# Moving the operand products of experts 1 and 2 and ScalarE's first copies ahead, and splitting a second stage of product 2 a third time

## The chip, the cores and the metric

The kernel runs on one core of a Trainium2 chip. The metric is device time in microseconds (us) of one execution; the median of several runs is compared. A profile of one execution comes with it.

The engines are named as the profile names them: PE is TensorE (matmul), DVE VectorE, ACT ScalarE, POOL GpSimd, SP SyncE. GpSimd and SyncE do little but issue transfers here, GpSimd those that cast float32 to float16.

## The reference

```python
"x": (16, 512, 512), "router_logits": (16, 512, 8), "expert_weights": (8, 512, 2048)   # float32
...
probs = np.exp(router_logits - logits_max)
probs = probs / np.sum(probs, axis=-1, keepdims=True)
for e in range(8):
    output += probs[:, :, e:e+1] * np.matmul(x, expert_weights[e])
```

A softmax over eight experts weighs eight matrix products of 8192 rows. Written as one product, row t of the left operand is the concatenation of p[t, e] * x[t] over the experts, 8 x 512 = 4096 long, and the right operand is the weights of all experts stacked, 4096 x 2048.

## The kernel before, in words

**Levels.** The big product is done in Strassen's way (Winograd's form), in up to three levels. The outer level splits the rows into even and odd blocks of 256, the experts into 0 to 3 and 4 to 7, and the columns into two halves of 1024; it makes seven products of the right operands (called product 1 to 7) for each of 16 pairs of row blocks. The inner level splits each of those again into seven steps, in the order 1, 5, 6, 2, 7, 3, 4; a step is eight matmuls of 128x128 weights by 128x512. The third level is used in some stages only: two such products are taken together (class `Third`), and steps 1 and 5 of both, 32 matmuls of 512 columns, become 14 parts of four matmuls of 256 columns. Its operands are sums that VectorE makes: `s`, four sums of 128x1024 from the left operands of both products, and `t`, sums of the weights, made once (class `Split`).

**Stages.** The work is cut into stages of two products each. Product 1 fills stages 0 to 4 and half of 5 to 8, product 2 the rest up to stage 14, and so on. A stage is split a third time where the program calls `third(stage, r)`: before the change stages 2, 3, 4 (product 1), stage 10 (product 2) and six stages of product 3. In such a stage TensorE does x1 x5 q1 q5, a step held over from the stage before, x2 q2 x6 q6, another one, x7 q7 x3 q3 x4 q4, and then the other steps. Of the third level's part 5, ScalarE copies the left 256 columns into a second bank and the right 256 into a tile `t5`, which VectorE adds back after parts 6 and 7.

**Operands and results.** The left operand z is xT * pT on VectorE, in float16; d are sums of z for the inner level, in a pool of three buffers (`spool`, tag "d"). Weights are cast by POOL's queue (L126) into `wpool`, 15 tiles. PSUM has eight banks, taken in turn by `bank()`. Results and copies of banks go through `hpool`, 13 tiles. SyncE's queue (L123) loads and stores.

**What sets the order.** VectorE and ScalarE always run in the order of the program. TensorE, POOL and SyncE do so from the place where `ordered[0]` is set, just ahead of stage 0; for what stands before it, a scheduler may interleave the instructions. In the stages a queue of VectorE's tasks is worked off by a planner with costs (`later(cost, make)`): TensorE's clock advances by 1.73 us a step, and tasks that a step needs are pulled forward.

**The start.** The first four half blocks of rows do not wait for transposed x: TensorE makes their operand itself. `diag_e(e)` (VectorE, L112) multiplies the identity by the probabilities of expert e, `early_z0(e, d, js)` multiplies x by those diagonals, 16 matmuls of 128x128 for one expert, into one bank for each j, and `evacuate` copies the banks out (VectorE at L238 for even j, ScalarE at L236 for odd). Then two column blocks (the loop over n) each take 64 matmuls, 16 for each of the four experts, into four banks, which ScalarE copies into h tiles (L335) and SyncE stores to `kept`. In the second block `early_xp1` makes transposes of further rows (matmuls by `ident`) and their probabilities (by `ones`). `softmax_of_all` makes the probabilities of all rows on VectorE, with one exponential on ScalarE (L184) and two casts there (L294, L295), and stores them to `p_dram`, from where the stages load pT.

The weights of the two column blocks come through POOL's queue in the order expert 0 (in two halves), 1, 2, 3 of the first block, experts 0 and 1 of the second, two blocks of x, and experts 2 and 3 of the second.

Of the kernel before, what the change touches and what calls it, by code (L numbers as in the profile page):

```python
# [31 lines left out]
def kernel(  # L32
# [7 lines left out]
    nc = tc.nc  # L40
    P = 128
    f16 = mybir.dt.float16
    f32 = mybir.dt.float32
# [4 lines left out]
    E, _, EH = expert_weights.shape  # L48
# [6 lines left out]
    HQ = 256  # L55
    NHQ = T // HQ
# [9 lines left out]
    spool = ctx.enter_context(tc.tile_pool(name="spool", bufs=3))  # L66
# [7 lines left out]
    def h_tile(shape, dtype):  # L74
        return hpool.tile(shape, dtype, name="h", tag="h")

    def half():
        return h_tile([P, NB], f32)
# [10 lines left out]
    with tc.tile_pool(name="psum0", bufs=1, space=bass.MemoryType.PSUM) as psum0:  # L89
        zero = wpool.tile([P, NB], f16, name="zero", tag="w")  # L90
# [9 lines left out]
    def note(i):  # L100
        last[i.ins.engine] = i.ins
        if ordered[0]:
            tc.keep_in_program_order(i)
# [5 lines left out]
    act = dve  # L109

    def tt(o, a, b, op):
        dve(nc.vector.tensor_tensor(out=o, in0=a, in1=b, op=op))  # L112
# [9 lines left out]
    def sp(o, i):  # L122
        note(nc.sync.dma_start(out=o, in_=i))  # L123
# [4 lines left out]
    def bank():  # L128
        return psum.tile([P, NB], f32, name="ps", tag="ps")

    def mm(ps, z, w, start, stop):
        note(nc.tensor.matmul(ps, z, w, start=start, stop=stop, skip_group_check=True))  # L132
# [3 lines left out]
    def new_w():  # L136
        return wpool.tile([P, K8, NB], f16, name="w", tag="w")
# [31 lines left out]
    def inner_sums(b, t7=None):  # L169

        w = {1: b[0, 0], 2: b[1, 0], 3: b[1, 1], 7: t7 or b[0, 1]}

        def step(p, x, y):
            if p not in w:
                w[p] = new_w()
            tt(w[p], x, y, SUB)
        return w, {5: lambda: step(5, b[0, 1], b[0, 0]), 6: lambda: step(6, b[1, 1], w[5]),
                   4: lambda: step(4, b[1, 0], w[6]), 7: lambda: step(7, b[1, 1], b[0, 1])}

    def softmax(lg, J, pf):  # L180
        mx = h_tile([P, J], f32)
        dve(nc.vector.tensor_reduce(out=mx, in_=lg, axis=AX, op=mybir.AluOpType.max))  # L182
        tt(lg, lg, mx.unsqueeze(2).to_broadcast([P, J, E]), SUB)
        nc.scalar.activation(out=lg, in_=lg, func=mybir.ActivationFunctionType.Exp)  # L184
        sm = h_tile([P, J], f32)
        dve(nc.vector.tensor_reduce(out=sm, in_=lg, axis=AX, op=ADD))  # L186
        dve(nc.vector.reciprocal(out=sm, in_=sm))  # L187
        n = pf.shape[1]
        tt(pf, lg.rearrange("p j e -> p e j")[:, 0:n], sm.unsqueeze(1).to_broadcast([P, n, J]), MUL)
        return pf  # L190
# [27 lines left out]
    def early_p(t):  # L218
        if t == 0:
            return softmax(lg0[t], 4, cpool.tile([P, HE, 4], f16, name="ph0"))  # L220
        pf = softmax(lg0[t], 4, cpool.tile([P, HE, 4], f32, name="pf0"))
        odd = pf.rearrange("p e (q j) -> p e q j", j=2)[:, :, :, 1]
        tt(odd[:, 0:2], odd[:, 0:2], odd[:, 2:4], ADD)
        ph = cpool.tile([P, HE, 4], f16, name="ph1")
        dve(nc.vector.tensor_copy(ph, pf))
        return ph

    def diag(p):

        d = h_tile([P, 4, P], f16)  # L230
        tt(d, ident.unsqueeze(1).to_broadcast([P, 4, P]), p.to_broadcast([P, 4, P]), MUL)
        return d

    def evacuate(o, ps, i):
        if i % 2:
            act(nc.scalar.copy(o, ps))  # L236
        else:
            dve(nc.vector.tensor_copy(o, ps))  # L238
# [4 lines left out]
    def diag_e(e):  # L243
        return diag(ph0[0][:, e].unsqueeze(2))

    def early_z0(e, d, js=range(4)):
        for j in js:
            ps = bank()
            for c in range(C):
                mm(ps[:, ds(c * P, P)], xs0[:, j, ds(c * P, P)], d[:, j], c == 0, c == C - 1)  # L250
            evacuate(z0[j][:, e], ps.rearrange("p (c t) -> p c t", c=C), j)
# [5 lines left out]
    def diag_j(j):  # L257
        return diag(ph0[1][:, :, ds(j % 4, 1)])

    def early_xp1(j, d):  # L260
        t, rows = j // 2 - 2, ds(j % 2 * P, P)
        ps = bank()
        for c in range(C):
            mm(ps[:, ds(c * P, P)], xs0[:, j, ds(c * P, P)], ident, c == 0, c == C - 1)
        evacuate(xp1[t][0][:, :, rows], ps.rearrange("p (c t) -> p c t", c=C), 0)
        ps = bank()
        mm(ps, ones, d.rearrange("p e t -> p (e t)"), True, True)
        evacuate(xp1[t][1][:, :, rows], ps.rearrange("p (e t) -> p e t", e=HE), 1)

    R = 4  # L270
    J = HQ // R
    p_dram = dram.tile([NHQ, 3 * HE, HQ], f16, name="p_dram")
# [3 lines left out]
    def load_logits():  # L276
        dve(nc.vector.memset(lg_all[:, 0, 0:1], 0.0))
        dve(nc.vector.memset(lg0[1][:, 0, 0:1], 0.0))
        for q in range(2):
            sp(lg0[1][:, ds(2 * q, 2), :], lg_f[ds((4 + 2 * q) * HQ, HQ)].rearrange("(j p) e -> p j e", p=P))  # L280
        for r in range(R):
            sp(lg_all[ds(r * NHQ, NHQ)], lg_v[r])

    def softmax_of_all():

        pf = softmax(lg_all, J, h_tile([P, E, J], f32))
        pq = h_tile([P, HE, J], f32)
        tt(pq, pf[:, 0:HE], pf[:, HE:E], ADD)
        low = ds(P // 2, P // 2)
        pv = pf.rearrange("p (s e) j -> p s e j", s=2)[low]  # L290
        tt(pv[:, :, 0:2], pv[:, :, 0:2], pv[:, :, 2:4], ADD)
        tt(pq[low, 0:2], pq[low, 0:2], pq[low, 2:4], ADD)
        ph = h_tile([P, 3 * HE, J], f16)
        act(nc.scalar.copy(ph[:, 0:E], pf))  # L294
        act(nc.scalar.copy(ph[:, E:], pq))  # L295
        for r in range(R):
            sp(p_dram[:, :, ds(r * J, J)], ph[ds(r * NHQ, NHQ)])

    kept = [dram.tile([2, HQ, NB], f32, name=f"kept_{i}") for i in range(NI)]

# [2 lines left out]
    ORDERS = [(c, j) for c in range(C) for j in range(4)], QUARTERS  # L303

    ds_ = [diag_e(0)]
    for h in range(2):
        early_z0(0, ds_[0], (2 * h, 2 * h + 1))
        for i in range(3 - 2 * h):
            mm(bank(), zero[:, 0:P], zero, True, True)
    load_logits()  # L310
    ds_ += [diag_e(1), diag_e(2)]
    for n in range(2):
        ps = [bank() for _ in range(4)]
        for e in range(HE):
            if n == 0 and e == 1:
                ds_.append(diag_e(3))
            if n == 0 and e == 2:
                ph0.append(early_p(1))
                ds_ = [diag_j(j) for j in range(4, 8)]
                softmax_of_all()  # L320
                w, sums = inner_sums(b11, new_w())
            for c, j in ORDERS[n == 0 and e == 0]:
                mm(ps[j], z0[j][:, e, c], b11[e // 2, n][:, e % 2 * C + c, :],
                   e + c == 0, e == HE - 1 and c == C - 1)
                ahead = {(0, 1, 3): 1, (0, 3, 3): 2, (1, 3, 3): 3}.get((e, c, j))
                if n == 0 and ahead:
                    early_z0(ahead, ds_[ahead])
            if n == 1:
                for j in ((4, 5), (6, 7), (), ())[e]:
                    early_xp1(j, ds_[j - 4])  # L330
                if e == 1:
                    sums[5]()
        for j in range(4):
            o = half()
            act(nc.scalar.copy(o, ps[j]))  # L335
            sp(kept[j // 2][n].rearrange("(p j) m -> j p m", j=2)[j % 2], o)

    ordered[0] = True
    SLOT = 1.73
# [37 lines left out]
    def evacuated(cost=0.61):  # L377
        clock["dve"] = max(clock["dve"], clock["pe"]) + cost
# [240 lines left out]
    class Third:  # L619
# [25 lines left out]
        def part(self, p, m):  # L645
            n = "xq"[THIRD.index(p)]
            if m == 1:
                self.b.banks[n] = bank()
            ya, yb = self.a.banks.get(n), self.b.banks[n]
            z, w = self.op(p, m), self.split.op(p, m)  # L650
            o = {1: (yb, 0), 5: (yb, 1), 2: (ya, 0), 6: (yb, 0), 7: (yb, 0), 3: (ya, 1), 4: (yb, 0)}[m]
            for c in range(C):
                mm(o[0][:, COLS[o[1]]], z[:, c], w[:, c], m == 1 and c == 0, c == C - 1)
            clock["pe"] += 0.44
            if m == 5:
                ya = self.a.banks[n] = bank()
                act(nc.scalar.copy(ya[:, COLS[0]], yb[:, COLS[0]]))
                self.t5[n] = h_tile([P, HQ], f32)
                act(nc.scalar.copy(self.t5[n], yb[:, COLS[1]]))
            elif m in (6, 7):  # L660
                evacuated(0.35)
                tt((ya if m == 6 else yb)[:, COLS[1]], yb[:, COLS[0]], self.t5[n], ADD)
# [552 lines left out]
    for stage in (2, 3, 4):  # L1215
        third(stage, 1)
    at(1, 2, splits[1].queue)
    for stage in (10,):
        third(stage, 2)
    at(9, 2, splits[2].queue)  # L1220

# [50 lines left out]
```

## Time and profile before

| | |
|---|---|
| median of three runs | 1371.24 us (1371.21 to 1373.33) |
| the profiled execution | 1371.77 us |
| its span in the trace | 1369.9 us |
| PE busy | 1360.8 us, 99% |
| DVE busy | 1122.1 us, 82% |
| POOL busy | 407.3 us, 30% |
| ACT busy | 194.7 us, 14% |
| chain that ended last | PE 98% |

The span runs from the first to the last recorded instruction of the profiled execution; 1.87 us of its time lie outside. Busy shares are averages over stages with different limits, so the rows that matter are those of the start and of single stages: what each engine did there and what ended its idle time.

### The profile page before, as it was taken

What the parts mean: (1) busy time and instruction counts of PE and PEld (TensorE: products, weight loads), DVE (VectorE), ACT (ScalarE), POOL (GpSimd) and SP (SyncE); (2) the same over time, 40 slices, a digit from 0 to 9 for tenths busy, and PEclk for the clock granted to TensorE, in tenths of its full rate; (3) what the DMA queues carried; (4) which work ended last, traced back from release to release, by engine and by line L of the source; (5) the groups of instructions that cost most, each with busy time, mean ns of one, the idle gap of its engine ahead of it and who ended that gap; (6) DMA issues with size and microseconds to landing.
All of it is one profiled execution on the core that took longest, in us unless ns stands there. A gap on an engine that the chain in (4) does not pass through costs nothing.

```text
span 1369.9 us, 18108 instructions
## 1 busy us (share of the span) xinstructions
PE 1360.8 (99%) x6634; PEld 645.9 (47%) x6634; DVE 1122.1 (82%) x1359; ACT 194.7 (14%) x358; POOL 407.3 (30%) x644
## 2 busy tenths in 40 slices
PE   8999999999999999999999999999999999999998
PEld 4455544454444444444444444444444444456554
DVE  5875867789889888788887888888889797898873
ACT  3232211100001111111111100000000000123221
POOL 3123324231223232333323122232332422223232
PEclk9999999999999999999999999999999999999999
DMA  9999999999897999999999978988798979989996
GB/s 181 205 239 230 249 241 280 289 289 367 265 327 231 335 327 306 256 286 310 306 271 343 339 257 222 210 240 203 228 256 222 247 203 291 306 205 239 208 204 119
DMA packets 191945, 353.79 MB, mean 258 GB/s; under 512 B 52976, under 2 KB 87024, under 8 KB 186736
## 3 DMA queue, kind: packets, MB, share of 16 engines
q0 software_dynamic: 88048, 183.02, 56.3%
q1 hardware_dynamic: 98048, 129.63, 31.0%
q10 hardware_dynamic: 5760, 39.99, 7.9%
q8 instruction: 52, 0.85, 0.3%
q14 instruction: 37, 0.30, 0.1%
HBM read 211.85 MB, written 167.97 MB: 277 GB/s over the span
## 4 chain that ended last, share of the span: by engine, by line
PE 98%; DVE 1%; DMA 1%; ACT 0%; issue 0%; POOL 0%; DVEq 0%; POOLq 0%
PE ps L132 98%; DMA w<-in_expert_weights_dram 1%; DVE h L112 0%; POOL w L126 0%; DVE z L112 0%; DVE z L238 0%; DVE h L186 0%; DVE h L187 0%; DVE h L182 0%; ACT h L184 0%; ACT h L294 0%; ACT h L335 0%; ACT h L1209 0%; DVE pf L112 0%; DVE ps L112 0%
## 5 line engine op out<-in xcount | busy, mean ns | idle before, releaser
L132 PE MATMUL ps<-w,z 128*128 128x512 f16 x5256 | 1131.2, 375 | 2.4 <-DMA w<-in_expert_weights_dram 2.4
L132 PEld LDWEIGHTS <-z 128*128 128x128 f16 x5336 | 521.9, 98 | 604.1 <-DVE h L112 2.7
L126 POOL DMA_DIRECT2D out_dram<-h x380 | 249.3, 663 | 746.2 <-ACT h L578 364.4
L112 DVE TENSOR_TENSOR h<-ps,h 128x512 f32<-128x512 f32 x415 | 284.5, 688 | 187.7 <-PE ps L132 169.8
L112 DVE TENSOR_TENSOR z<-xT,pT 128x2048 f16<-128x2048 f16 x216 | 262.2, 1217 | 6.6 <-DMA xT<-w 4.8
L132 PE MATMUL ps<-w,d 128*128 128x512 f16 x880 | 199.1, 379 | 0.0
L132 PEld LDWEIGHTS <-d 128*128 128x128 f16 x880 | 86.1, 98 | 101.7
L112 DVE TENSOR_TENSOR z<-z,d 128x2048 f16<-128x2048 f16 x110 | 131.5, 1217 | 0.0
L578 ACT COPY h<-ps 128x512 f32<-128x512 f32 x64 | 37.5, 586 | 503.7 <-PE ps L132 499.2
L112 DVE TENSOR_TENSOR w<-w 128x1024 f16<-128x1024 f16 (+2 forms) x88 | 99.9, 1146 | 1.8 <-PE ps L132 1.0
L567 ACT COPY h<-ps 128x512 f32<-128x512 f32 x90 | 52.7, 586 | 309.2 <-PE ps L132 297.1
L112 DVE TENSOR_TENSOR ps<-ps,h 128x512 f32<-128x512 f32 (+1 forms) x106 | 62.2, 591 | 23.8 <-PE ps L132 23.2
L112 DVE TENSOR_TENSOR d<-z 128x1024 f16<-128x1024 f16 x110 | 74.6, 687 | 4.2 <-PE ps L132 2.8
L564 ACT COPY h<-ps 128x512 f32<-128x512 f32 x90 | 51.9, 589 | 142.0 <-PE ps L132 132.4
L126 POOL DMA_DIRECT2D kept<-h x56 | 30.9, 552 | 102.6 <-ACT h L567 74.3
L126 POOL DMA_DIRECT2D w<-in_expert_weights_dram x65 | 48.8, 782 | 20.1 <-DMA wd<-w 8.4
L126 POOL DMA_DIRECT2D wd<-w x78 | 44.3, 593 | 32.9 <-DVE w L112 27.6
L112 DVE TENSOR_TENSOR u<-xT,pT 128x2048 f16<-128x2048 f16 x38 | 46.2, 1217 | 0.0
L112 DVE TENSOR_TENSOR h<-h 128x512 f32<-128x512 f32 (+2 forms) x69 | 45.1, 675 | 0.1
L112 DVE TENSOR_TENSOR z<-z,u 128x2048 f16<-128x2048 f16 x34 | 41.4, 1217 | 0.1
L560 ACT COPY ps<-ps 128x512 f32<-128x512 f32 x45 | 25.6, 570 | 99.6 <-PE ps L132 93.8
L112 DVE TENSOR_TENSOR z<-z 128x2048 f16<-128x2048 f16 x32 | 39.1, 1222 | 0.7
(61 smaller groups left out, 278.7 us busy)
## 6 DMA issues: line engine op xcount, KB each, us to landing
out_dram<-h POOLq DMA_DIRECT2D x380, 256.0 KB, 6.9
pT<-p_dram SPq DMA_DIRECT2D x125, 256.0 KB, 6.8
h<-kept SPq DMA_DIRECT2D x108, 256.0 KB, 7.2
w<-wd ACTq DMA_DIRECT2D x25, 1024.0 KB, 8.9
xT<-x SPq DMA_DIRECT2D x74, 256.0 KB, 6.8
w<-in_expert_weights_dram POOLq DMA_DIRECT2D x35, 512.0 KB, 9.9
wd<-w POOLq DMA_DIRECT2D x64, 256.0 KB, 6.5
h<-out_dram SPq DMA_DIRECT2D x60, 256.0 KB, 5.4
```

Source lines behind the costliest of these rows:

```text
L112: dve(nc.vector.tensor_tensor(out=o, in0=a, in1=b, op=op))
L126: note(nc.gpsimd.dma_start(out=o, in_=i, **how))
L132: note(nc.tensor.matmul(ps, z, w, start=start, stop=stop, skip_group_check=True))
L560: act(nc.scalar.copy(self.banks["b"], x))
L564: act(nc.scalar.copy(o[tn], q if p == 5 else x))
L567: act(nc.scalar.copy(o[TN[p]], b if p == 2 else x))
L578: act(nc.scalar.copy(o[tn], b))
```

## The change

1. `early_z0` of experts 1 and 2, with the diagonals, moves ahead of the first column block; before, each expert's 16 matmuls stood between matmuls of the block. Those of expert 3 move to the place before expert 1's matmuls of the block. One filler matmul on zeros is left out (three stay).
2. `early_p(1)`, the next diagonals and `softmax_of_all` move from ahead of expert 2 to ahead of expert 1 of the first block. `softmax_of_all` now returns a function, `keep`, with ScalarE's two casts and SyncE's four stores to `p_dram`; it is called after the first block's four bank copies and stores, so that these come first on ScalarE and on SyncE.
3. Stage 11 is split a third time as stage 10 is.
4. `t5` is no longer taken from `hpool`, one tile for each of two banks, but from the pool of "d", as one tile with both halves. This holds for every stage that is split a third time.

```diff
         ph = h_tile([P, 3 * HE, J], f16)
-        act(nc.scalar.copy(ph[:, 0:E], pf))
-        act(nc.scalar.copy(ph[:, E:], pq))
-        for r in range(R):
-            sp(p_dram[:, :, ds(r * J, J)], ph[ds(r * NHQ, NHQ)])
+
+        def keep():
+            act(nc.scalar.copy(ph[:, 0:E], pf))
+            act(nc.scalar.copy(ph[:, E:], pq))
+            for r in range(R):
+                sp(p_dram[:, :, ds(r * J, J)], ph[ds(r * NHQ, NHQ)])
+        return keep
...
     ds_ = [diag_e(0)]
-    for h in range(2):
-        early_z0(0, ds_[0], (2 * h, 2 * h + 1))
-        for i in range(3 - 2 * h):
-            mm(bank(), zero[:, 0:P], zero, True, True)
+    early_z0(0, ds_[0], (0, 1))
+    for i in range(3):
+        mm(bank(), zero[:, 0:P], zero, True, True)
+    ds_.append(diag_e(1))
+    early_z0(0, ds_[0], (2, 3))
     load_logits()
-    ds_ += [diag_e(1), diag_e(2)]
+    for e in (1, 2):
+        ds_.append(diag_e(e + 1))
+        early_z0(e, ds_[e])
     for n in range(2):
         ps = [bank() for _ in range(4)]
         for e in range(HE):
             if n == 0 and e == 1:
-                ds_.append(diag_e(3))
-            if n == 0 and e == 2:
+                early_z0(3, ds_[3])
                 ph0.append(early_p(1))
                 ds_ = [diag_j(j) for j in range(4, 8)]
-                softmax_of_all()
+                keep_p = softmax_of_all()
                 w, sums = inner_sums(b11, new_w())
             for c, j in ORDERS[n == 0 and e == 0]:
                 mm(ps[j], z0[j][:, e, c], b11[e // 2, n][:, e % 2 * C + c, :],
                    e + c == 0, e == HE - 1 and c == C - 1)
-                ahead = {(0, 1, 3): 1, (0, 3, 3): 2, (1, 3, 3): 3}.get((e, c, j))
-                if n == 0 and ahead:
-                    early_z0(ahead, ds_[ahead])
...
             sp(kept[j // 2][n].rearrange("(p j) m -> j p m", j=2)[j % 2], o)
+        if n == 0:
+            keep_p()
...
-                self.t5[n] = h_tile([P, HQ], f32)
+                if not self.t5:
+                    t = spool.tile([P, 2, HQ], f32, name="d", tag="d")
+                    self.t5 = {"x": t[:, 0], "q": t[:, 1]}
...
-    for stage in (10,):
+    for stage in (10, 11):
         third(stage, 2)
```

## The prediction

> **What bounds the kernel now.** I read the page first, then TensorE's waits, then the timelines of the start and of stages 10 and 11.
>
> ```profile
> PE 1360.8 (99%) x6634; PEld 645.9 (47%) x6634; DVE 1122.1 (82%) x1359; ACT 194.7 (14%) x358; POOL 407.3 (30%) x644
> PE 98%; DVE 1%; DMA 1%; ACT 0%; issue 0%; POOL 0%; DVEq 0%; POOLq 0%
> ```
> ```profile
> PE ps L132 <- ACT h L335: 1.4, 1, 1.4
> PE ps L132 <- DVE ps L112: 0.2, 1, 0.2
> ```
>
> TensorE is busy 1360.8 us of a span of 1369.9 us and carries 98% of the chain that ended last. Only two things can shorten this kernel: less matmul time, and the waits at the start. Behind the start TensorE waits once, 0.2 us for VectorE, so what the start gains stays gained unless something later takes it back.
>
> Timelines of the start (start, duration, engine, form, count, idle before and its releaser): first TensorE, then VectorE and ScalarE.
>
> ```profile
> 7.53 0.38 PE L132 MATMUL ps<-zero 128*128 128x512 f16 x1
> 10.28 1.89 PE L132 MATMUL ps<-w,z 128*128 128x512 f16 x8 [2.37 <-DMA w<-in_expert_weights_dram]
> ...
> 18.97 1.06 PE L132 MATMUL ps<-h,w 128*128 128x128 f16 x16
> 19.86 10.52 PE L132 MATMUL ps<-w,z 128*128 128x512 f16 x48
> 31.76 0.38 PE L132 MATMUL ps<-ident,w 128*128 128x128 f16 x4 [1.37 <-ACT h L335]
> ...
> 37.04 8.15 PE L132 MATMUL ps<-w,z 128*128 128x512 f16 x37
> ```
> ```profile
> 7.51 0.69 DVE L238 CAST z<-ps 128x512 f16<-128x512 f32 x1 [0.70 <-PE ps L132]
> 8.13 0.69 DVE L112 TENSOR_TENSOR h<-ident,ph 128x512 f16<-128x512 f16 x1
> ...
> 20.60 0.18 DVE L182 TENSOR_REDUCE h<-lg 128x4 f32<-128x32 f32 x1
> ```
> ```profile
> 30.21 0.62 ACT L294 CAST h<-h 128x512 f16<-128x512 f32 x1 [3.37 <-DVE h L112]
> 31.04 2.04 ACT L335 COPY h<-ps 128x512 f32<-128x512 f32 x4
> ```
>
> Two idle stretches stand out: 2.37 us before the first weights, and the one before 31.76, where early_xp1 needs a bank that ScalarE has not copied out. The 48 matmuls from 19.86 are issued by 30.22 (48 x 0.2158 us, the pitch of 96 matmuls in 20.72 us in the stage rows below), so that gap is 1.54 us. ScalarE's copies begin only at 31.04, since the casts of the softmax stand ahead of them and wait for VectorE's chain, which began at 20.60.
>
> **The start, step by step.** One expert's early_z0 is 16 matmuls, 19.86 - 18.97 = 0.89 us of TensorE. Those of experts 1 and 2 now run in the idle stretch. Expert 1's diagonals (one VectorE operation of 0.69) come between expert 0's two casts and are done by the second one's start at 7.51; expert 2's, now at 8.13, are done at 8.8. So expert 1 runs 7.55 to 8.44 and expert 2 8.87 to 9.76, before 10.28. This takes 2 x 0.89 = 1.78 us off the path. The filler that goes (7.53) lies in idle time: nothing. Expert 3's 0.89 us only moves, to behind expert 0's block.
>
> Late next could be the weights. The casting queue shows when a block lands, by when it wakes (its idle, and the block that released it):
>
> ```profile
> 11.73 0.76 POOL L126 DMA_DIRECT2D w<-in_expert_weights_dram  x1 [0.57 <-DMA w<-in_expert_weights_dram]
> 14.47 0.74 POOL L126 DMA_DIRECT2D w<-in_expert_weights_dram  x1 [1.98 <-DMA w<-in_expert_weights_dram]
> 17.59 0.70 POOL L126 DMA_DIRECT2D w<-in_x_dram  x1 [2.38 <-DMA w<-in_expert_weights_dram]
> 21.09 0.71 POOL L126 DMA_DIRECT2D w<-in_x_dram  x1 [2.80 <-DMA w<-in_expert_weights_dram]
> 23.29 0.71 POOL L126 DMA_DIRECT2D w<-in_x_dram  x1 [1.49 <-DMA w<-in_expert_weights_dram]
> 25.83 0.72 POOL L126 DMA_DIRECT2D w<-in_x_dram  x1 [1.83 <-DMA w<-in_expert_weights_dram]
> ```
>
> In this order they are the second half of expert 0, then experts 1, 2, 3, and experts 0 and 1 of the second column block. TensorE's new needs, with 16 matmuls as 3.45 us: expert 0 10.28 (second half 12.0), expert 3's operand 13.73, expert 1 14.63, expert 2 18.08, expert 3 21.53, then 24.98 for the second block. Each has landed, with 0.2 to 1.7 us in hand, the least for expert 1. TensorE ends the second block's expert 0 at 28.44.
>
> There early_xp1 needs the banks. VectorE's softmax chain begins about when expert 3's casts end, 15.4 instead of 20.6, and ScalarE's exponentials come 5.2 us earlier with it (the logits came in by q1 at 13 to 15 us, in a row below). ScalarE's four copies, 2.04 us in all, can start when the first block is full, at 24.98, and are over by 27; the casts come behind them. So the 1.54 us go as well and nothing waits at 28.44. Stage 0, now at 37.04 + 32 x 0.2158 = 43.95, starts at 40.63: **-3.32 us**.
>
> What moves with it, on SyncE's queue: the four kept stores are issued at about 25 to 28, ahead of the four p_dram stores. Shown here are the stores of before, SyncE's first loads of p_dram, and what the casting queue (q0) and SyncE's (q1) moved in windows of the trace: 13 to 15, 33 to 34, 35 to 36 and 38 to 39 us (packets, MB, share of the engines):
>
> ```profile
> 31.16 2.71 SPq L123 DMA_DIRECT2D p_dram<-h  x4
> 33.96 2.76 SPq L123 DMA_DIRECT2D kept<-h  x4
> ```
> ```profile
> 45.95 1.24 SPq L123 DMA_DIRECT2D pT<-p_dram  x2
> ```
> ```profile
> q0 software_dynamic: 301, 0.30, 89.2%
> q1 hardware_dynamic: 302, 0.19, 40.9%
> ```
> ```profile
> q0 software_dynamic: 209, 0.21, 124.1%
> ```
> ```profile
> q0 software_dynamic: 158, 0.15, 87.5%
> q1 hardware_dynamic: 463, 0.06, 45.1%
> ```
> ```profile
> q1 hardware_dynamic: 292, 0.40, 106.9%
> ```
>
> The stores issued from 31.16 moved nothing at 33 to 34, while the casting queue filled the engines, and began at 35. If that holds, the second block's last weights are not delayed: with 2.5 us a block (23.29 to 25.83) and half that for each x block between, experts 2 and 3 land at about 30.9 and 33.4, and are needed at 33.7 and 37.2. I take nothing. The other bound: the kept stores (1 MB at 0.40 MB a us, 2.6 us) and the p_dram stores (within 35 to 38, partly shared: an estimate of 2.6 us) go ahead of the weights in full, expert 2 lands at 36.1 and TensorE stands 2.4 us. That p_dram is written later than the kept tiles costs nothing: the first loads from it are issued at 45.95, after the shift at 42.6, and the stores are out by about 38.
>
> **Stage 11.** Stage 10, split a third time already, against stage 11, which is plain:
>
> ```profile
> 280.28 0.60 PE L132 MATMUL ps<-t,s 128*128 128x256 f16 x4
> ...
> 289.41 3.62 PE L132 MATMUL ps<-w,d 128*128 128x512 f16 x16
> 292.86 20.88 PE L132 MATMUL ps<-w,z 128*128 128x512 f16 x96
> 313.58 3.62 PE L132 MATMUL ps<-w,d 128*128 128x512 f16 x16
> ```
>
> From 280.28 to 289.41 TensorE does 52 of the 56 matmuls of 256 columns and two held slots of eight 512s, 3.45 us: 5.68/52 = 0.109 us each, 6.1 us for 56. The plain form is 32 x 0.2158 = 6.9 us. Splitting stage 11 takes **-0.8 us**.
>
> For it VectorE gets four operand sums of 1024 (0.69) and four adds of 256 (0.43), 4.5 us, and ScalarE two pairs of small copies. VectorE's rows and its busy time around the stage (windows of 10 us: length, then TensorE, its weight loads, VectorE and so on; the sum is over 290 to 350), and a row of VectorE's timeline in stage 12:
>
> ```profile
> L112 DVE TENSOR_TENSOR d<-z 128x1024 f16<-128x1024 f16 x110 | 74.6, 687 | 4.2 <-PE ps L132 2.8
> L112 DVE TENSOR_TENSOR ps<-ps,h 128x256 f32<-128x256 f32 x42 | 17.7, 431 | 23.0 <-PE ps L132 22.9
> ```
> ```profile
> 300.00:310.00 10.00, 10.00 (x48) 4.58 (x47) 8.55 (x12) 0.00 (x0) 3.81 (x7) 1.00 1.10 332
> 310.00:320.00 10.00, 10.00 (x48) 4.52 (x47) 10.00 (x13) 0.59 (x1) 0.38 (x2) 1.00 1.07 348
> sum 60.00, PE 60.00 PEld 27.20 DVE 54.91 ACT 3.52 POOL 13.47; mean PE 10.00 PEld 4.53 DVE 9.15 ACT 0.59 POOL 2.24
> ```
> ```profile
> 319.13 4.61 DVE L112 TENSOR_TENSOR w<-w 128x4096 f16<-128x4096 f16 x2
> ```
>
> Over 60 us VectorE is idle 5.1 us, against 4.5 added, and it is full from 310 to 320. What can give way are the weight sums of 128x4096, two of them in the last row and a third soon behind, which are for later stages: the changed program has them one by one between evacuations, some 8 us later. The narrowest place is the end of the third level, where parts x4 and q4 write banks that VectorE must have read for the adds behind x7 and q7: walking the new order at the durations shown, each of these adds ends 0.3 to 0.5 us before TensorE wants its bank, an estimate. I take no stall; the bounds are 0 and the whole 4.5 us.
>
> **The small pool.** The part t5 now takes one of three buffers of "d" in every third stage and gives two h buffers free. In the order of VectorE the buffers' last readers are past when ScalarE writes it, so I take nothing; the bounds are -0.2 us (the one wait for VectorE above) and the price of the last rival.
>
> **Sum.** -3.3 - 0.8 = -4.1 us. The profiled run took 1371.77 us, 1.87 outside its span, and would be 1367.6; it lies 0.5 above the median of 1371.24, so the forecast against the median is **1367.1 us**.
>
> **Rivals.**
> The stores collide. The kept stores share the DMA engines with the weights from 25 us on. For it: at 13 to 15 and at 35 to 36 both queues move at once. Against it: nothing of theirs moved in the window at 33. TensorE waits between 0.5 and 2.4 us, 1367.6 to 1369.5; the middle is 1368.6. [...]
>
> VectorE is full. Of its 4.5 us in stage 11 some land on TensorE: half of them makes 1369.3, all 1371.6.
>
> The start gains less than it says. If the weights, not TensorE, set the pace (expert 1 has only 0.2 us in hand), the 1.78 us turn into waits for weights and only the 1.54 and 0.8 remain: 1368.9.
>
> Slower: the small pool. If ScalarE, in its order, stands for a "d" buffer that TensorE still reads, both third-level banks are copied late. One held slot of eight matmuls, 1.73 us, lost in each of the eleven third stages is 19 us: 1386. It decides from 0.6 us a stage, where the 4.1 are eaten and 2.7 more. Against it: the order of the buffers above. Half a slot makes 1376.6.
>
> **How the numbers follow.** A run tells this kernel from no change by about 0.2%, 2.7 us, so faster means under 1368.5. The forecast has bounds of its own: 0.5 below, as far as the profiled run and the median lie apart, and the 0.2 of the pool; 0.5 above for the same, and 0.4 for short waits where the margins were 0.2 to 0.5. That is 1366.4 to 1368.0, and it gets 0.60. The stores get 0.13, half of it under 1368.5; VectorE 0.10, a third under; the start's weights 0.09, a third under; the small pool 0.08. Faster 0.60 + 0.065 + 0.035 + 0.03 = 0.73, same 0.19, slower 0.08. The range, 1366.4 to 1370.2, leaves out the small pool, the upper third of VectorE's case and a little below.
>
> **What would show it.** Right: no idle of TensorE before 31, early_xp1 at about 28.4, stage 0 at 40.6; ScalarE's first copies ahead of its casts; 256-column rows in stage 11, and the start of stage 12 some 4.1 us earlier than now; waits of TensorE for VectorE at 0.2 us still. Wrong: a wait of TensorE for weights between 14 and 38 us (the stores, or the pace), a wait for VectorE at about 309 to 325 (VectorE full), or small waits for ScalarE or VectorE in every third stage (the pool).

## The result, and the profile after

The changed kernel takes 1368.86 us, the median of ten runs (1367.32 to 1369.89), against 1371.41 us for ten runs of the kernel before. The ratio is 0.998, with a 95% interval from 0.9971 to 0.9989: faster by 2.55 us, inside the forecast range, where 4.1 were forecast. It lies above 1368.0, the top of the prediction's own bounds, and above 1368.5, its line for faster, though the interval leaves out 1. The profiled run took 1369.08 us, its span 1367.1.

The start came out as forecast. TensorE's timeline of the start after the change, then ScalarE's (columns as before):

```profile
6.82 1.58 PE L132 MATMUL ps<-h,w 128*128 128x128 f16 x24
8.62 1.07 PE L132 MATMUL ps<-h,w 128*128 128x128 f16 x16 [0.22 <-DVE h L112]
10.26 3.63 PE L132 MATMUL ps<-w,z 128*128 128x512 f16 x16 [0.57 <-DMA w<-in_expert_weights_dram]
13.72 1.06 PE L132 MATMUL ps<-h,w 128*128 128x128 f16 x16
14.61 13.98 PE L132 MATMUL ps<-w,z 128*128 128x512 f16 x64
28.43 0.39 PE L132 MATMUL ps<-ident,w 128*128 128x128 f16 x4
...
33.64 11.60 PE L132 MATMUL ps<-w,z 128*128 128x512 f16 x53
```
```profile
24.53 2.05 ACT L337 COPY h<-ps 128x512 f32<-128x512 f32 x4 [2.94 <-PE ps L132]
26.44 0.65 ACT L296 CAST h<-h 128x512 f16<-128x512 f32 x1
```

Experts 1 and 2 run before the first weights, which leaves 0.57 us of the idle stretch, expert 3 runs at 13.72, and the 64 matmuls behind it find all their weights. early_xp1 begins at 28.43 without a wait; 28.44 was forecast. Stage 0 begins at 33.64 + 32 x 0.2158 = 40.55 us, 3.40 earlier.

TensorE from stage 10 on after the change:

```profile
286.01 3.62 PE L132 MATMUL ps<-w,d 128*128 128x512 f16 x16
...
300.26 0.60 PE L132 MATMUL ps<-t,s 128*128 128x256 f16 x4
...
309.39 3.62 PE L132 MATMUL ps<-w,d 128*128 128x512 f16 x16
...
318.14 17.45 PE L132 MATMUL ps<-w,z 128*128 128x512 f16 x80 [1.68 <-DVE z L112]
```

From 286.01 to 309.39 are 23.38 us; before, the same stretch took 313.58 - 289.41 = 24.17. The split saves 0.79 us, as forecast. But the row at 318.14 is new: TensorE waits 1.68 us for an operand z, that of step 7 of stage 11. Where VectorE was, and the chain of waits there:

```profile
309.76 1.28 DVE L112 TENSOR_TENSOR h<-ps,h 128x512 f32<-128x512 f32 x2
316.26 0.69 DVE L112 TENSOR_TENSOR h<-ps,h 128x512 f32<-128x512 f32 x1 [5.22 <-DMA h<-kept]
316.87 1.22 DVE L112 TENSOR_TENSOR z<-z,d 128x2048 f16<-128x2048 f16 x1
```
```profile
305.66 1.23 DVE z L112
...
306.90 0.32 SPq L123
...
307.31 8.83 DMA h<-kept
...
316.26 0.69 DVE h L112
316.95 1.14 DVE z L112
...
318.14 1045.34 PE ps L132 x5016
```

VectorE was not overloaded: it stood idle for 5.22 us, for a kept tile that it adds to a result of stage 11, and the operand z came behind that add in its order. Reading the chain upwards: the kept tile landed at 316.14, 8.83 us after its load was issued at 307.31. SyncE issued it right behind a pT load at 306.90, and that one had waited for VectorE to finish a z at 306.88 and so free the tile. SyncE's queue in the changed kernel and, in the second fence, in the kernel before (about 3.4 us later on its clock):

```profile
292.21 0.42 SPq L123 DMA_DIRECT2D xT<-x  x1
303.08 0.32 SPq L123 DMA_DIRECT2D pT<-p_dram  x1
303.45 0.42 SPq L123 DMA_DIRECT2D xT<-x  x1
306.90 0.32 SPq L123 DMA_DIRECT2D pT<-p_dram  x1
307.31 12.50 SPq L123 DMA_DIRECT2D h<-kept  x9
```
```profile
289.94 19.05 SPq L123 DMA_DIRECT2D h<-kept  x8
309.04 0.44 SPq L123 DMA_DIRECT2D xT<-x  x1
309.57 0.46 SPq L123 DMA_DIRECT2D pT<-p_dram  x1
```

Before, ten kept loads (eight of them in the lines above) stand between one group of loads of xT and pT and the next; now there are eight, and two have come to stand behind. The program does that. A stage that precedes a split one holds its last two steps over into it, and what hangs on a step is held over with it. The loads of one kept tile for each product of stage 11 hang on the last step but one of stage 10 (step 12, counted from 0). When stage 11 became a split stage, they moved behind the place where stage 11 asks for the xT and pT of stage 13. The two loads for stage 10 were held over in the same way before the change, without harm: in its profile the first was issued at 280.39, 11 us ahead of its add at 291.34. So being held over is not enough; the loads must also be late behind what stands ahead of them.

### The profile page after: what moved, and what is told of

It reads as the page before. It is cut to its first block, busy times and chain, and to the rows that moved or that the text cites. A ratio compares the mean times of both kernels' runs of the same rounds, so it can differ in the third digit from the quotient of the medians.

```text
span 1367.1 us, 18164 instructions
## 1 busy us (share of the span) xinstructions
PE 1359.5 (99%) x6657; PEld 648.1 (47%) x6657; DVE 1125.3 (82%) x1367; ACT 195.9 (14%) x362; POOL 407.4 (30%) x644
## 4 chain that ended last, share of the span: by engine, by line
PE 98%; DMA 1%; DVE 0%; POOL 0%; issue 0%; ACT 0%; SPq 0%; POOLq 0%; DVEq 0%
PE ps L132 98%; DMA h<-kept 1%; DMA w<-in_expert_weights_dram 1%; DVE z L112 0%; POOL w L126 0%; DVE h L112 0%; DVE ps L112 0%; ACT h L1215 0%; SPq L123 0%; POOL ident L202 0%; DVEq L112 0%; POOLq L202 0%; POOLq L1262 0%
## 5 line engine op out<-in xcount | busy, mean ns | idle before, releaser
L112 DVE TENSOR_TENSOR ps<-ps,h 128x512 f32<-128x512 f32 (+1 forms) x66 | 45.1, 686 | 4.3 <-PE ps L132 4.0
```

## The experiments

Theory A is SyncE's order: the kept loads are late because of what stands ahead of them. Rivals are VectorE's load (B), late landing by shared DMA engines (C), and, for the start, which of its moves did the work. Times are medians, each beside the kernel before on the same chip.

**e1, the kept loads one step earlier.**

```diff
-        for slot, tn in zip((8, 10, 12, 13), INNER):
+        for slot, tn in zip((8, 10, 11 if k == 11 else 12, 13), INNER):
```

> The changed kernel, with one edit: the two loads of the kept tiles that step 6 of stage 11 adds to are issued one slot earlier in stage 10, so that on SyncE's queue they stand ahead of the four xT and pT loads for stage 13 and no longer behind them. VectorE's, ScalarE's and TensorE's order is the same. Theory A (SyncE's order: two pT loads wait for tiles that VectorE frees at 303.05 and 306.88, the kept loads stand behind them, VectorE stands 5.2 us and TensorE 1.7): the wait of TensorE at 318 goes, 1368.9 - 1.7 = 1367.2 us, and the runs lie closer together. Theory B (VectorE has too much to do in stage 11, with whatever it waits for): another operation is late in its place, 1368.5 to 1369. Theory C (the kept loads land late, 8.8 us, because the queues share the engines): they land as late but are issued earlier; the time is as by A, and the duration from issue to landing stays at 8 to 9 us.

1367.23 us (1366.37 to 1367.97) against 1371.10, ratio 0.9967 (0.9955 to 0.998). All of TensorE's waits in its profile:

```profile
PE every L94 <- DVE zero L91: 1.3, 1, 1.3
PE ps L132 <- DMA w<-in_x_dram: 0.9, 1, 0.9
PE ps L132 <- DVE h L112: 0.2, 1, 0.2
```

The wait for z is gone with nothing changed but the place of two loads on SyncE's queue. VectorE does the same operations in the same order, and over 290 to 350 us it is now busier (56.72 us against 52.56 of 60, because it no longer stands still), so B falls for stage 11. SyncE's two loads in e1, then VectorE's adds of the two tiles:

```profile
302.25 0.32 SPq L123 DMA_DIRECT2D h<-kept  x1
...
305.13 0.32 SPq L123 DMA_DIRECT2D h<-kept  x1
```
```profile
311.11 0.69 DVE L112 TENSOR_TENSOR h<-ps,h 128x512 f32<-128x512 f32 x1 [0.28 <-PE ps L132]
...
312.85 0.69 DVE L112 TENSOR_TENSOR h<-ps,h 128x512 f32<-128x512 f32 x1
```

They land after 6.4 and 5.8 us, at 308.7 and 310.9, so 2.5 and 1.9 us are in hand. In the changed kernel it was the first of the two that VectorE stood for, issued at 307.31 and landed at 316.14. So the gain has two parts: the load is issued 5.1 us earlier, and it lands in 6.4 us in place of 8.8. The first part would nearly do alone, since 302.25 + 8.83 = 311.08. Theory C had the landing stay at 8 to 9 us, and it did not; why it is shorter is not shown. In e1 no pT load holds the two back any more: SyncE waits 10.0 us ahead of the first and 2.5 us ahead of the second for stores to the output, which free the h tiles that the loads fill.

**e11 and e12, the same two kernels side by side.** No edits to the changed kernel and to e1.

> The changed kernel as it is, side by side with the next one on one chip, since the gain of the earlier kept loads (1.6 us, from different calls) is not much more than the spread of its runs. Theory A: 1368.9 us, runs spread over some 2.5 us, because the wait depends on when the late kept loads land; 1.6 us above the next kernel.

> The kernel with the kept loads issued earlier, e1 unchanged, on the same chip. Theory A: 1367.2 us, runs within 1.6 us, no wait of TensorE for VectorE above 0.3 us. If the difference was between chips or runs: the same as the kernel beside it, 1368 to 1369.

1368.69 us (eleven runs) and 1367.19 us (twelve runs) against 1370.99: ratios 0.9986 (0.9978 to 0.9995) and 0.9978 (0.9969 to 0.9986). The difference of 1.50 us holds on one chip: the two intervals overlap, but ten of the twelve runs of e1 lie below all eleven of the changed kernel. The profiles differ as in A: 0.9 us in two waits for z in the changed kernel, none in e1. That wait was 1.7 us in one profile of the changed kernel and 0.9 in the other, which fits a wait set by a landing.

**e2, stage 11 not split.**

```diff
-    for stage in (10, 11):
+    for stage in (10,):
         third(stage, 2)
```

> The changed kernel without the third split of stage 11 (the start and the small pool as changed). If the start's gain is 3.3 to 3.4 us and all of it stays, 1371.4 - 3.4 = 1368.0 us, which is faster than the whole change, and the split then costs 0.8 to 0.9 net. If part of the start's gain is taken back later on whether stage 11 is split or not (a load that lands at its own time, whatever TensorE does), there is a wait of about 1.7 us in this kernel too: 1369.7.

1367.97 us against 1371.10, a ratio of 0.9977 (0.9967 to 0.9986): 3.1 us from the start and the small pool alone, and no wait for z. The start's gain stays whole. Against 1368.86 the split as made cost 0.9 us net (0.6 with each kernel against the kernel before beside it; the intervals overlap), and with e1's order it brings 0.7.

**e3, the split alone.** The kernel before with `for stage in (10, 11)`.

> The kernel before with stage 11 split a third time and nothing else (the part t5 stays in the pool of h). Theories A and B: -0.8 for the matmuls and +1.7 for TensorE's wait, 1371.4 + 0.9 = 1372.3 us. If the wait comes from what the earlier start shifts (transfers that now collide), it is not here: 1370.6.

1373.92 us (1372.03 to 1376.0), a ratio of 1.0018 (1.0009 to 1.0027): slower than before, by 2.8 us and not by 0.9. Three of TensorE's waits in its profile:

```profile
PE ps L132 <- DVE z L112: 1.5, 1, 1.5
PE ps L132 <- ACT h L335: 1.4, 1, 1.4
...
PE ps L132 <- ACT h L659: 1.0, 1, 1.0
```

The wait for z is there without the earlier start, so nothing that the start shifts causes it. New is the row of L659, ScalarE's copy of t5 into an h tile, which the next two kernels take up. The -0.8 and the two waits make 1.7 of the 2.8 us; where the rest lies is not shown. This profile was also slowed by the clock in its start, told at the end.

**e4, t5 back in the pool of h.**

```diff
-                if not self.t5:
-                    t = spool.tile([P, 2, HQ], f32, name="d", tag="d")
-                    self.t5 = {"x": t[:, 0], "q": t[:, 1]}
+                self.t5[n] = h_tile([P, HQ], f32)
```

> The changed kernel with the part t5 back in the pool of h, one tile for each bank, in every stage that is split a third time. If the move costs and brings nothing, as the prediction took it: 1368.9 us. If it was needed, because two stages split in a row want more h tiles than there are and SyncE's kept loads wait for them: TensorE's wait in stage 12 grows, by 1 to 3 us, 1370 to 1372. If the small pool costs in each of the eleven stages: faster than 1368.4.

1370.14 us (1367.43 to 1371.67), 1.3 above the changed kernel. The profiled run was the fastest of them and shows no wait of TensorE for it, so this kernel alone settles nothing; e9 does.

**e9, e1 with t5 back in the pool of h.** The same edit on e1.

> The kernel with the kept loads issued earlier (e1), and t5 back in the pool of h in every third stage. With t5 in h, ScalarE's copies of it waited for stores of h tiles in stage 11: 2.17 and 1.62 us in the profile of the split alone, where TensorE then waited 1.0 us for ScalarE, and 1.2 and 1.3 us in that of the changed kernel with t5 in h, without a wait of TensorE. Theory S (the small pool is what keeps these copies on time, whatever SyncE does): ScalarE waits again, 1 to 2.5 us, and the median is 0.3 to 1.5 above e1: 1367.5 to 1368.7. Theory A alone (the excess of that kernel, 1370.1 against 1368.9, came through SyncE's order too): 1367.2.

1370.85 us (1368.33 to 1371.86): 3.6 us above e1, more than either theory expected. The profiled run took 1369.63, 2.4 above e1. ScalarE's timeline in stage 11, then TensorE's row:

```profile
300.96 0.36 ACT L661 COPY ps<-ps 128x256 f32<-128x256 f32 x1 [7.19 <-PE ps L132]
305.59 0.37 ACT L663 COPY h<-ps 128x256 f32<-128x256 f32 x1 [4.27 <-DMA out_dram<-h]
305.86 0.38 ACT L661 COPY ps<-ps 128x256 f32<-128x256 f32 x1
```
```profile
306.29 0.60 PE L132 MATMUL ps<-w,z 128*128 128x256 f16 x4 [2.33 <-ACT ps L661]
```

The copy of t5 waits 4.27 us for an h tile whose store to the output has not landed, the copy of the second bank stands behind it in ScalarE's order, and TensorE waits 2.33 us for that bank. In the chain this store takes 11.45 us to land. The move to the small pool, which the prediction took at nothing, is what makes a split of stage 11 pay: theory S. The 2.33 us account for the profiled run; what the median has beyond them is not shown, and seven of the eleven runs had a mean granted clock of 0.998 or 0.999.

**e5, the casts first again (on e1).**

```diff
-                keep_p = softmax_of_all()
+                softmax_of_all()()
...
-        if n == 0:
-            keep_p()
```

> The kernel with the kept loads issued earlier (e1), and ScalarE's two casts and the p_dram stores back ahead of the first four bank copies. Theory P (the products of experts 1, 2 and 3, made earlier, bring VectorE's softmax chain forward to 15.4, and that alone ends the wait of early_xp1): the chain ends at 25.1, the casts at 26.2, the first bank is free by 26.7, before 28.4; 1367.2 us, no wait before 31. Theory O (the order of ScalarE's queue is what ended it): the wait comes back in part or in full, 1367.7 to 1368.8.

1367.74 us (1366.94 to 1368.13), a ratio of 0.9968 (0.9955 to 0.998), within the spread of e1. ScalarE's start, then TensorE's:

```profile
24.54 0.62 ACT L296 CAST h<-h 128x512 f16<-128x512 f32 x1 [3.37 <-DVE h L112]
...
25.37 2.04 ACT L337 COPY h<-ps 128x512 f32<-128x512 f32 x4
```
```profile
28.01 0.39 PE L132 MATMUL ps<-ident,w 128*128 128x128 f16 x4
```

The casts come before the copies, and early_xp1 still starts without a wait. Theory P holds here: once expert 3's product and the softmax are early, VectorE's chain ends by 24.5 and ScalarE's order does not matter.

**e6, the products late again (on e1).** The start as in the kernel before, with `keep_p` behind the four copies.

> The kernel with the kept loads issued earlier (e1), with the products of experts 1, 2 and 3, the filler and the softmax back in their old places in the start; the four bank copies still come ahead of the casts. Theory O: the copies start when the block is full, at 26.7, early_xp1 finds its banks at 30.2, and only the 1.8 us of products in the idle stretch are lost: 1367.2 + 1.8 = 1369.0 us. Theory P: the wait of 1.5 us comes back as well: 1370.5.

1368.84 us (1368.51 to 1370.71), ratio 0.9983 (0.9974 to 0.9992); theory O gave 1369.0.

```profile
26.38 2.03 ACT L338 COPY h<-ps 128x512 f32<-128x512 f32 x4
29.84 0.62 ACT L296 CAST h<-h 128x512 f16<-128x512 f32 x1 [1.44 <-DVE h L112]
```
```profile
29.86 0.39 PE L132 MATMUL ps<-ident,w 128*128 128x128 f16 x4
```

Here VectorE's chain ends as late as before, 29.8, but the copies no longer stand behind the casts, and TensorE does not wait. So either move alone ends the 1.54 us, and the two together do it once. The products themselves are worth 1368.84 - 1367.23 = 1.6 us (1.4 with each against the kernel before beside it); 1.78 was worked out.

**e7, the kernel before without its fillers.**

```diff
-        for i in range(3 - 2 * h):
-            mm(bank(), zero[:, 0:P], zero, True, True)
```

> The kernel before without its four filler matmuls on zeros (1.2 us, in idle time), which leaves TensorE idle for longer ahead of the first weights. If idle time is all that the fillers fill: 1371.1 us as before. If the slower cluster of the runs of before (some 2 us above the rest) comes from the granted clock, which was 0.50 at 12 to 14 us in the profile of the split alone and 1.00 in that of before, and idle time brings it on: the clock falls in the profile of this kernel, between 10 and 16 us, and most runs lie in the slower cluster, 1373.0 us.

1373.25 us (1371.97 to 1374.75) against 1371.35, ratio 1.001 (1.0001 to 1.0019): about 2 us more for 1.2 us less work, and the clock fell as the second theory has it. The windows of 10 to 12 and 12 to 14 us (the number behind POOL's count is the granted clock):

```profile
10.00:12.00 2.00, 1.85 (x5) 0.68 (x5) 0.00 (x0) 0.00 (x0) 1.05 (x2) 0.59 1.24 206
12.00:14.00 2.00, 2.00 (x12) 1.09 (x11) 0.02 (x1) 0.00 (x0) 0.43 (x1) 0.56 1.34 217
```

**e8, three stages split in a row (on e1).** `for stage in (10, 11, 12)`, with stage 12's two kept loads one step earlier too.

> The kernel with the kept loads issued earlier (e1), with stage 12 split a third time as well and its two kept loads issued early too. If VectorE can hold three such stages in a row: another 0.8 us, 1366.4. If it is full by then (it was 91% busy over these 60 us before, and each split adds 4.5 us in 23): TensorE waits for VectorE in stage 12 or 13, 1367.2 to 1369.

1368.91 us (1368.56 to 1369.97), 1.7 above e1. VectorE's timeline in stage 12, then TensorE's row:

```profile
335.81 2.28 DVE L112 TENSOR_TENSOR w<-w 128x4096 f16<-128x4096 f16 x1
...
338.61 2.28 DVE L112 TENSOR_TENSOR w<-w 128x4096 f16<-128x4096 f16 x1
340.81 2.35 DVE L112 TENSOR_TENSOR z<-z,d 128x2048 f16<-128x2048 f16 x2
```
```profile
342.08 17.44 PE L132 MATMUL ps<-w,z 128*128 128x512 f16 x80 [1.74 <-DVE z L112]
```

Here VectorE does not stand still; it works on two weight sums while TensorE waits for z. It looks like the rival "VectorE is full", one split later than it was feared; the next kernel tells whether it is.

**e10, two weight sums one stage later (on e8).**

```diff
-        for make in (make1, make3, make2):
-            later(2.2, make)
+        later(2.2, make1)
+        at(12, 6, lambda: [later(2.2, make) for make in (make3, make2)])
```

> The kernel with three stages split in a row (e8), with the second and third of the weight sums of 128x4096 queued one stage later (stage 12, step 6, in place of stage 11, step 6). In e8 these two, 2.28 us each, stood ahead of the operands of steps 7 and 3 of stage 12, and TensorE waited 1.74 us for them. If that order is what made VectorE late: the wait goes and the split of stage 12 pays, 1368.9 - 1.7 = 1367.2, or with the gap to e1 closed in full 1366.4 us. If VectorE simply has too much to do: the wait moves to stage 13, where four such sums now stand ahead of the same operands, 1368 to 1370.

1367.07 us (1366.84 to 1367.58), ratio 0.9967 (0.9954 to 0.9979). The wait of 1.74 us is gone, so the order of the sums made it, and not a lack of time on VectorE. But the kernel is no faster than e1 (1367.23) by more than the runs spread: in the profiles stage 12's stretch shrank from 24.17 us to 23.85 and not to 23.4, with one wait of 0.25 us for VectorE listed in it in place of the large one. A third split in a row gives about nothing back. e1 and e10 are the fastest versions found.

## Why the prediction was right, and where it was off

**The start, -3.3: right.** The profile shows 3.40, e2 3.1. Two products of 0.89 and the wait of 1.54 were the terms. The step "the casts come behind them. So the 1.54 us go as well" was right in its end, but the change did this twice: e5 and e6 show that the earlier chain or ScalarE's new order would each have sufficed.

**The weights and the stores: right in the end, with a wrong reason.** No wait for weights came. But the reason, that SyncE's stores move nothing while the casting queue is busy, fell. The queues in the window from 29 to 30 us after the change:

```profile
q0 software_dynamic: 97, 0.10, 56.0%
q1 hardware_dynamic: 95, 0.19, 55.8%
```

The stores, issued from 25.14 on, moved nothing until 28, and from 29 on they shared the engines with the weights: 95 packets beside 97 in this window, 55.8% of the engines beside 56.0%. So the empty window at 33 to 34 before the change reads as a late start of the stores: there, too, nothing of theirs moved for some 4 us after 31.16. Why they start late is not shown. The weights did come later: experts 2 and 3 of the second block, which landed at 30.6 and 33.2 before the change, landed at 31.4 and 35.7 (issued at 11.77 and 14.54, 19.6 and 21.2 us to landing). TensorE wanted them at 33.64 and 37.09. What saved the forecast were the margins of 2.8 and 3.8 us that it had worked out, of which 2.3 and 1.4 were left.

**Stage 11, -0.8: mis-sized, +0.9.** The matmul term was right, 0.79. The step that failed is "I take no stall": it went through VectorE's order and asked whether VectorE had the time, and it had. It did not go through SyncE's queue, which the held steps take with them. That cost 1.7 us in the profile; e1 gives it back by order alone. The prediction's own sign of being wrong, a wait for VectorE at about 309 to 325, came at 318. The rival "VectorE is full" that it stood for had the right place and nearly the right price (half of its 4.5 us), but the wrong cause: e1 ends the wait with VectorE busier than before, and even the wait in e8, one split later, goes with the order of the sums (e10).

**The small pool, 0: mis-sized.** That it would cost nothing was right, and the slower rival built on it did not show: ScalarE's copies into "d" wait for nothing (0.0 us of idle time ahead of all 22 in the changed kernel's profile). But the bound of -0.2 us for its gain was far off. It was taken from the kernel before, where the copies into h do not wait (0.0 us ahead of all 20); with two split stages in a row they do (4.27 us in e9). By e4 and e9 the move is worth 1.3 to 3.6 us, of which the profile of e9 shows 2.33 as a wait.

**The sum.** -3.4 for the start, -0.8 for the matmuls, +1.7 for the wait makes -2.5; measured are -2.55. That the time lies in the forecast range is in part luck: the range reached up to 1370.2 for stalls by the stores, the weights or a full VectorE, and the stall that came had a cause that is none of these.

## What to carry to other kernels

When work is moved or held over, follow each transfer that hangs on it through its queue: here a kept load stood on SyncE's queue behind a pT load that went out at 306.90, was issued at 307.31 in place of 302.25 (e1), and the wait of 1.68 us that came of it was listed as TensorE's for VectorE. When an idle row on VectorE names a transfer, look at when that transfer was issued before looking at how long it took. And where a stage is made denser, ask of each pool not how it fared before, but when its tiles come free if two such stages follow each other.

## What the runs showed of the hardware

In some runs TensorE's granted clock fell after the idle stretch ahead of the first weights. In the profile of the kernel before it was 1.00 at 12 to 14 us; in that of e3, with the same start, it was 0.50 there, and 16 matmuls of 128x128 took 1.71 us from start to start of the next group in place of 0.89:

```profile
12.43 1.91 PE L132 MATMUL ps<-h,w 128*128 128x128 f16 x16
14.14 2.31 PE L132 MATMUL ps<-w,z 128*128 128x512 f16 x8
```

In windows of 2 us from 10 to 16 us the clock was 0.89, 0.50 and 0.75 in e3, and 0.59, 0.56 and 1.00 in e7, where the fillers are gone. What each window lacks of 1.00, times its 2 us, adds up to 1.7 us in either, an estimate from these windows alone; e7 is 1.9 us longer. Over whole runs the mean granted clock was under 1.000 in all eleven runs of e7, and in six of the 26 runs of the kernel before beside it; five of these six took 1373.0 to 1373.7 us, against their median of 1371.35. So with the fillers, 1.2 us of matmuls on zeros in idle time, 20 of 26 runs kept a mean of 1.000, and without them none of eleven.

The length of the idle stretch alone does not decide it. The clock fell after 1.98 us of it in e3 and 2.27 us in e7, with 0.78 and 0.45 us of idle time a little ahead; it did not fall after 2.37 us in the profile of the kernel before. What else decides it is not shown. In the profiles of the changed kernel, where 0.57 us of idle time or less are left, the clock stayed at 1.00 there. The earlier products do not rule a lower clock out: single runs of the changed kernel in e11 and of e1 in e12 had a mean of 0.998 or 0.999 (those of 1372.93 and 1372.65 us among them), and no profile shows where.

A store from the casting queue took 11.45 us to land in e9, where the median of these stores was 6.9 us in the profile before; the tile it held stopped ScalarE for 4.27 us of it.
